# A seven-product scheme for two of the four GLU column passes in both S5 layers of a four-layer trunk

## The chip, the cores and the metric

The kernel runs on one core of a Trainium2 chip. The time is the device time of one execution in microseconds; the figure to compare is the median of several runs. The profile is one execution of its own, whose time is given beside its span below.

## What is computed

The reference is a trunk of four layers over 512 tokens of width 1024. Layers 0 and 3 use the S5 mixer, layer 1 gated linear attention, layer 2 differential attention, and every layer is followed by a SwiGLU feed-forward block (FFN). What matters here is the end of the S5 mixer, a gated linear unit (GLU):

```python
    z = jax.nn.gelu(y).astype(h.dtype)      # 512 tokens x 1024
    a, b = jnp.split(z @ w_glu, 2, axis=-1) # w_glu is 1024 x 2048
    return a * jax.nn.sigmoid(b)
...
        x = x + mix.astype(x.dtype)
        h = rmsnorm(x, norm_ffn[layer])
        x = x + swiglu_ffn(h, ffn_w_gate_up[layer], ffn_w_down[layer]).astype(x.dtype)
```

The sigmoid is computed as half of one plus a tanh of half the argument.

## The kernel before

**Numbers in two parts.** Each fp32 operand is held as a high part (a cast to fp32r, by ScalarE) and a low part (what the cast left over, by VectorE). One product of two operands is three matmuls (`mm3`): high by high, high by low, low by high. The mixer's output `zT` lies transposed in SBUF, 8 blocks of 128 rows, 512 tokens wide, both parts.

**Passes.** `w_glu` has four column groups of 512: the left ones (`a`) at 0 and 512, the gate ones (`b`) at 1024 and 1536. A pass is one `gemm_b`: four accumulators (one bank of PSUM for each 128 tokens), the inner dimension taken in four blocks of 256 rows. For every block `wb` loads 128x1024 numbers (512 KB) into a staging tile `wst` (three buffers), `high` (L368, ScalarE) and `low` (L376, VectorE) make a `whl` tile (five buffers), and 24 matmuls of 128x512 follow (L396 to L398). Pass b0 (columns 1024 to 1535) is done inside the S5 pipeline, a step behind it. `s5_glu` (L1866) then does a0, b1 and a1. `evac_b` is the tanh of the gate pass on ScalarE (L1878); `evac_a` multiplies and adds into the residual `x`, two VectorE operations for each 128 tokens (L1881, L1883).

**What follows.** `nxt` is a `Sides`, the left operand of the next FFN. `take(t, d)` takes 128 tokens and one half of the width once `x` is complete there: it lets earlier tiles go through `put` (four PE transposes, L123, then `keep`, four ScalarE scalings, L211, and after the second tile `parts`, L206 and L207) and squares the rows (L114). `flush` issues all puts that are pending. In the last pass `gemm_b` runs with `tail=4`: the last four blocks of 128 rows are done token tile by token tile, so that the tiles finish one behind another. `ahead(2)` loads and splits the first two weight blocks of the FFN ("heads"), and `total("3")` makes one of the FFN's own left sums (L225).

**The FFN's own scheme.** The FFN multiplies gate and up halves by a seven-product scheme: both operands are cut in quarters, and seven products of quarters with sums and differences of quarters take the place of eight. `seven_block` makes its sums of weights by an accumulating DMA from the POOL queue (L601) or by a VectorE addition (L658). Its first weights go to `slots`, to a `lent` tile, to `wst` and to the spare gain tile `left.g`.

**Order.** Outside `hand_all()` a planner orders each engine's instructions from the program's order and its own estimate of when they are ready. From `hand_all()` to `hand()` each engine (PE, ScalarE, VectorE, POOL and SP, which issues the DMAs) keeps the order as it is written. Each engine takes its instructions strictly in order, so a waiting one holds up those behind it. Tiles of a new pool share memory with tiles of a pool that has ended and wait until those were last used.

## Time and profile before

| what | value |
|---|---|
| runs | 2285.26, 2279.61, 2278.34 us, median 2279.61 us |
| the profiled execution | 2281.29 us, its span 2279.4 us |
| granted TensorE clock | 0.991 of full speed |
| GLU of layer 0, three passes in `s5_glu` | about 163 to 232 us of the span |
| GLU of layer 3, the same three passes | about 1861 to 1931 us of the span |
| median weight load of `w_glu` in layer 0, from issue to landing | 4.4 us |

The profile lists instructions by source line and engine, and a line may belong to a helper: L368 and L376 serve every weight split of the kernel, so one stage is read by asking for a window of time. The start times of matmuls tell their rate; their durations overlap, because the next one starts before the last has drained. What an engine waited for stands in square brackets behind its idle time.

### The profile page before, as it was taken

Reading aid. Unit: us, or ns where it says so; the run is one execution under the profiler, and the core shown is the slowest. Engines: PE = TensorE matmul, PEld = TensorE weight load, DVE = VectorE, ACT = ScalarE, POOL = GpSimd, SP = SyncE. Lnnn points to the kernel's source line nnn. Section 1 sums busy time; section 2 is a strip of 40 time slices with the busy share of each in tenths; the row PEclk is TensorE's granted clock in tenths of the full one; section 3 lists DMA queues with packets and bytes.
Section 4 is the critical chain, followed back from the end, with each engine's and each line's share of the span. In section 5 each row is a group of like instructions: output and inputs, shape, how many; then the busy total and the mean of one; then the engine's idle time right before and its main releaser. Section 6 shows DMA issues by size and latency. Waiting matters only on the chain.

```text
span 2279.4 us, 37223 instructions
## 1 busy us (share of the span) xinstructions
PE 2204.5 (97%) x14847; PEld 1956.4 (86%) x14847; DVE 1560.5 (68%) x2420; ACT 1120.6 (49%) x1870; POOL 281.6 (12%) x392
## 2 busy tenths in 40 slices
PE   5899999999999999999999999999999899999997
PEld 3778979899877799998988887999998788989896
DVE  8873887776624469777754675977766964957574
ACT  6533645454453456555535676744444234635342
POOL 1000140522000010101002231101000000101000
PEclk9999999999999999999999999999999999999999
DMA  4247475663422457765336365885631646767521
GB/s 88 46 134 194 113 188 159 181 185 99 123 65 74 131 133 202 184 166 172 96 129 145 89 150 154 238 216 135 179 94 38 159 137 157 191 161 177 154 77 65
DMA packets 295463, 317.83 MB, mean 139 GB/s; under 512 B 72221, under 2 KB 235353, under 8 KB 294906
## 3 DMA queue, kind: packets, MB, share of 16 engines
q1 hardware_dynamic: 233050, 234.23, 34.1%
q0 software_dynamic: 62240, 81.22, 19.1%
q8 instruction: 117, 1.92, 0.3%
q14 instruction: 56, 0.46, 0.1%
HBM read 283.54 MB, written 16.65 MB: 132 GB/s over the span
## 4 chain that ended last, share of the span: by engine, by line
PE 81%; DVE 9%; ACT 4%; issue 2%; DMA 2%; SPq 1%; POOL 0%; ACTq 0%; DVEq 0%; POOLq 0%
PE a L565 17%; PE acc L396 14%; PE acc L398 13%; PE acc L397 13%; PE c L565 8%; PE d L565 4%; PE y L1481 2%; DVE whl L376 2%; ACT whl L368 1%; PE V L1445 1%; PE s L2306 1%; PE op L2340 1%; PE tp L123 1%; DMA wst<-in_ffn_w_gate_up_dram 1%; DVE halves L229 1%
## 5 line engine op out<-in xcount | busy, mean ns | idle before, releaser
L376 DVE TENSOR_TENSOR whl<-wst,whl 128x1024 fp32r<-128x1024 f32 x272 | 331.6, 1224 | 260.2 <-ACT whl L368 259.4
L368 ACT CAST whl<-wst 128x1024 fp32r<-128x1024 f32 x272 | 283.9, 1050 | 310.0 <-PE acc L398 221.8
L565 PE MATMUL a<-side,whl 128*128 128x256 f32 x3168 | 382.5, 277 | 4.2 <-DVE whl L376 3.6
L565 PEld LDWEIGHTS a<-side,whl 128*128 128x128 f32 x3168 | 369.4, 188 | 6.9 <-DVE whl L376 5.3
L396 PE MATMUL acc<-whl,act 128*128 128x512 f32 x704 | 278.3, 396 | 1.3 <-DVE x L548 1.3
L397 PE MATMUL acc<-whl,act 128*128 128x512 f32 x704 | 274.7, 390 | 0.0
L398 PE MATMUL acc<-whl,act 128*128 128x512 f32 x704 | 274.6, 390 | 0.0
L565 PE MATMUL c<-side,whl 128*128 128x256 f32 x2112 | 254.3, 277 | 1.2 <-DVE whl L376 1.2
L565 PEld LDWEIGHTS c<-side,whl 128*128 128x128 f32 x2112 | 246.7, 188 | 2.0 <-DVE whl L376 2.0
L376 DVE TENSOR_TENSOR whl<-slot,whl 128x1024 fp32r<-128x1024 f32 x107 | 130.5, 1223 | 70.2 <-ACT whl L368 70.2
L396 PEld LDWEIGHTS acc<-whl,act 128*128 128x128 f32 x704 | 132.1, 188 | 31.7 <-issue 2.2
L398 PEld LDWEIGHTS acc<-whl,act 128*128 128x128 f32 x704 | 132.1, 188 | 28.1
L397 PEld LDWEIGHTS acc<-whl,act 128*128 128x128 f32 x704 | 132.2, 188 | 25.5
L368 ACT CAST whl<-slot 128x1024 fp32r<-128x1024 f32 x107 | 112.2, 1053 | 83.9 <-PE acc L398 35.1
L396 PE MATMUL acc<-whl,hT 128*128 128x512 f32 x352 | 142.8, 406 | 0.0
L398 PE MATMUL acc<-whl,hT 128*128 128x512 f32 x352 | 138.3, 393 | 0.0
L397 PE MATMUL acc<-whl,hT 128*128 128x512 f32 x352 | 138.2, 393 | 0.0
L565 PE MATMUL a<-sides,whl 128*128 128x256 f32 x1056 | 134.3, 283 | 0.0
L565 PEld LDWEIGHTS a<-sides,whl 128*128 128x128 f32 x1056 | 129.7, 191 | 1.0
L565 PE MATMUL d<-sides,whl 128*128 128x256 f32 x1056 | 126.6, 276 | 1.0 <-ACT whl L368 1.0
L565 PEld LDWEIGHTS d<-sides,whl 128*128 128x128 f32 x1056 | 122.9, 188 | 1.2 <-ACT whl L368 1.2
L704 ACT CAST act<-r 128x512 fp32r<-128x512 f32 (+1 forms) x110 | 66.3, 646 | 115.2 <-DVE r L683 107.9
(458 smaller groups left out, 3877.3 us busy)
## 6 DMA issues: line engine op xcount, KB each, us to landing
wst<-in_ffn_w_gate_up_dram SPq DMA_DIRECT2D x88, 512.0 KB, 4.8
wst<-in_ffn_w_down_dram SPq DMA_DIRECT2D x88, 512.0 KB, 4.2
slot<-in_ffn_w_gate_up_dram SPq DMA_DIRECT2D x71, 512.0 KB, 5.6
wst<-in_ffn_w_gate_up_dram POOLq DMA_DIRECT2D x44, 512.0 KB, 6.3
halves<-in_ffn_w_gate_up_dram SPq DMA_DIRECT2D x43, 512.0 KB, 5.3
wst<-in_s_w_glu_dram SPq DMA_DIRECT2D x32, 512.0 KB, 4.5
wst<-in_gla_w_in_dram SPq DMA_DIRECT2D x24, 512.0 KB, 3.6
wst<-in_diff_w_qkv_dram SPq DMA_DIRECT2D x24, 512.0 KB, 4.2
```

What stands on the lines that cost most here:

```text
L123: tr.nc.tensor.transpose(p[:, j], h[:, j * P : (j + 1) * P], tr.ident[:])
L229: v.tensor_tensor(s, s, y, op=op)
L368: self.last["high"] = self.nc.scalar.copy(hl[:, 0], w[:])
L376: self.last["low"] = self.nc.vector.tensor_tensor(hl[:, 1], w[:], hl[:, 0].bitcast(F32), op=ALU.subtract)
L396: mm(out, lh, rh, start=first, stop=False)
L397: mm(out, lh, rl, start=False, stop=False)
L398: self.last["mm"] = mm(out, ll, rh, start=False, stop=last)
L565: mm(o, hl[:, x, k, c], side[y][:, k], start=first and not (j or k or n), stop=k == 3 and n == 2, skip_group_check=True,)
L704: self.last["act high"] = nc.scalar.copy(dst[:, 0, j], src[:, j])
L1445: mm(V[kk][z][:, bs(b)], inm[:, z, bs(b)], U[:, bs(b)], start=True, stop=True)
L1481: mm(yb[:, b], q[:, j, b], om[:, j // 2, bs(b)], start=False, stop=j == 3)
L2306: nc.tensor.matmul(ss[m][:], qs[:, m, ts], ks[:, m, z], start=z == 0, stop=z == 1)
```

## The change

Pass a0 stays a pass of eight blocks of rows, now with four callbacks between its blocks. The work of b1 and a1 becomes seven products. The left operand is cut in quarters of 256 tokens by 512 inner rows (names "11", "12" for the first 256 tokens, "21", "22" for the others), the weights in quarters of 512 inner rows by 512 columns (a group, then b group).

`WideSides` makes the left sums. `whole` joins high and low parts of "21", "22" and "11" on POOL, each 128x1024 numbers ("11" in two tiles of 512). `first` to `third`, beside pass a0, make sides "1", "2" and "3", and `fourth`, behind product five, side "4". `second` also joins "12". The tile `s` of these sums is the spare gain tile, which the FFN later uses for a weight.

`seven_wide` makes the weight sums. T (`wsum`, 128x2048) is loaded, has a second quarter added by a POOL DMA, and is later changed twice by VectorE additions (`total`). Weights "3" are a staged load with an accumulating POOL DMA on top. Each product is 24 matmuls of 128x512: two token tiles, four inner blocks, three matmuls. The products run in the order one, five, six, two, seven, three, four. Results move between PSUM banks and SBUF rows r1, r5 and r2 as in the FFN's scheme. Token tiles 0 and 1 are complete before product four, tiles 2 and 3 by it. `hand_all()` now stands behind the split of weights "4".

```diff
--- before.py
+++ after.py
@@ -241,6 +241,64 @@
         for ks, y in self.of(name):
             hi, lo = (z[:, ks] for z in self.place[name])
             self.tr.nc.vector.tensor_tensor(lo, y, hi.bitcast(F32), op=ALU.subtract)
+class WideSides:
+    def __init__(self, tr, pool, hT, spare):
+        self.tr, self.hT = tr, hT
+        self.m = pool.tile([P, 4, 256], F32, name="summand")
+        self.y = {n: pool.tile([P, 2, 4, 256], F32R, name="wide" + n) for n in ("1", "4", "3", "2")}
+        self.s = spare[:].rearrange("p (k n) -> p k n", n=256)
+    def quarter(self, name, z):
+        th, kh = int(name[0]) - 1, int(name[1]) - 1
+        return self.hT[:, z, 4 * kh : 4 * kh + 4, th * 256 : (th + 1) * 256]
+    def stat(self, name):
+        y = (lambda z: self.quarter(name, z)) if len(name) == 2 else (lambda z: self.y[name][:, z])
+        return lambda k, z, t: y(z)[:, k, t * P : (t + 1) * P]
+    def joined(self, out, name, ks=slice(0, 4)):
+        hi, lo = (self.quarter(name, z)[:, ks].bitcast(F32) for z in range(2))
+        self.tr.nc.gpsimd.tensor_tensor(out, hi, lo, op=ALU.add)
+    def parts(self, name, src, ks=slice(0, 4)):
+        hi, lo = (self.y[name][:, z, ks] for z in range(2))
+        self.tr.nc.scalar.copy(hi, src)
+        self.tr.nc.vector.tensor_tensor(lo, src, hi.bitcast(F32), op=ALU.subtract)
+    def whole(self):
+        self.u = [(slice(k, k + 2), self.tr.np_.tile([P, 2, 256], F32, tag="hh", name="wideu")) for k in (0, 2)]
+        self.joined(self.s, "21")
+        self.joined(self.m[:], "22")
+        for ks, u in self.u:
+            self.joined(u[:], "11", ks)
+    def first(self):
+        v = self.tr.nc.vector
+        for ks, u in self.u:
+            v.tensor_tensor(u[:], u[:], self.s[:, ks], op=ALU.subtract)
+        v.tensor_tensor(self.s, self.s, self.m[:], op=ALU.subtract)
+        self.parts("1", self.s)
+    def second(self):
+        for ks, u in self.u:
+            self.tr.nc.vector.scalar_tensor_tensor(
+                self.s[:, ks], u[:], -1.0, self.m[:, ks], op0=ALU.mult, op1=ALU.subtract
+            )
+        self.joined(self.m[:], "12")
+        self.parts("2", self.s)
+    def third(self):
+        for ks, u in self.u:
+            self.parts("3", u[:], ks)
+    def fourth(self):
+        self.tr.nc.vector.tensor_tensor(self.s, self.s, self.m[:], op=ALU.add)
+        self.parts("4", self.s)
 
 
 class Chunks:
@@ -551,6 +609,103 @@
 
         return evac
 
+    def seven_wide(self, w, cols, sums, T, four, r2):
+        nc = self.nc
+        v = nc.vector
+        mm = nc.tensor.matmul
+        piece = lambda q, half, b: self.wb_src(w, 4 * q + 2 * b, cols[half])
+        r1, r5 = four[:2], four[2:]
+        a, c = ([self.acc() for z in range(2)] for y in range(2))
+        f = {"r1": r1, "r5": r5, "a": a}
+        H = {}
+        def load(q, half, plus=None):
+            out = []
+            for b in range(2):
+                y = self.staged(piece(q, half, b), 2, 512)
+                if plus:
+                    nc.gpsimd.dma_start(y[:], piece(*plus, b), accum_op=ALU.add)
+                out.append(y)
+            return out
+        def split(name, ys):
+            H[name] = [self.halves(y, 2, 512) for y in ys]
+        cut = lambda b: T[:, 2 * b : 2 * b + 2]
+        def total(q, half):
+            for b, y in enumerate(load(q, half)):
+                v.tensor_tensor(cut(b), cut(b), y[:], op=ALU.add)
+        def product(side, name, bank, first, tiles=(0, 1), ks=slice(0, 4)):
+            st = sums.stat(side)
+            for t in tiles:
+                for k in range(4)[ks]:
+                    hl = H[name][k // 2]
+                    for n, (x, y) in enumerate(((0, 0), (0, 1), (1, 0))):
+                        mm(
+                            bank[t][:], st(k, x, t), hl[:, y, k % 2], start=first and not (k or n),
+                            stop=k == 3 and n == 2, skip_group_check=True,
+                        )
+        for b in range(2):
+            nc.sync.dma_start(cut(b), piece(0, 1, b))
+            nc.gpsimd.dma_start(cut(b), piece(0, 0, b), accum_op=ALU.add)
+        split("11", load(0, 0))
+        def one():
+            split("1", [cut(0), cut(1)])
+            product("11", "11", a, True)
+            for z in range(2):
+                nc.scalar.copy(r1[z][:], a[z][:])
+        def five():
+            total(1, 1)
+            split("2", [cut(0), cut(1)])
+            product("1", "1", c, True)
+            for z in range(2):
+                nc.scalar.copy(r5[z][:], c[z][:])
+        def six():
+            split("21", load(1, 0))
+            product("2", "2", a, False)
+            for z in range(2):
+                nc.scalar.copy(r2[z][:], a[z][:])
+        def two():
+            d = [self.sbank("d") for z in range(2)]
+            split("3", load(0, 1, (1, 1)))
+            product("12", "21", d, True)
+            for z in range(2):
+                v.tensor_tensor(r1[z][:], r1[z][:], d[z][:], op=ALU.add)
+        def seven():
+            split("22", load(1, 1))
+            product("3", "3", a, False)
+        def seven_out(z):
+            v.tensor_tensor(r5[z][:], r5[z][:], a[z][:], op=ALU.subtract)
+        def three():
+            total(1, 0)
+            product("4", "22", c, False)
+        def three_out(z):
+            v.tensor_tensor(r2[z][:], c[z][:], r2[z][:], op=ALU.subtract)
+        def four_weights():
+            split("4", [cut(0), cut(1)])
+        def four(z, ks=slice(0, 4)):
+            product("22", "4", a, False, (z,), ks)
+        return dict(
+            f, one=one, five=five, six=six, two=two, seven=seven, seven_out=seven_out, three=three, three_out=three_out,
+            four=four, **{"four weights": four_weights},
+        )
 
     def seven_product(self, side, w, bank, first, hl=None):
 
@@ -1870,28 +2025,58 @@
         wg = self.i["s5_w_glu"][L]
         nxt = Sides(self, 3 * L, self.i["ffn_w_gate_up"][3 * L])
         with self.tc.tile_pool(name=f"s5g_{L}", bufs=1) as p:
-            for d in range(2):
-                gate = [None] * NT
-
-                def evac_b(t, ps):
-                    gate[t] = p.tile([P, 512], F32, tag="gate", name="gate", bufs=6)
-                    nc.scalar.activation(gate[t][:], ps[:], AF.Tanh, scale=0.5)
-
-                def evac_a(t, ps):
-                    v.scalar_tensor_tensor(gate[t][:], gate[t][:], 1.0, ps[:], op0=ALU.add, op1=ALU.mult)
-                    xs = self.x[:, t, d * 512 : (d + 1) * 512]
-                    v.scalar_tensor_tensor(xs, gate[t][:], 0.5, xs, op0=ALU.mult, op1=ALU.add)
-                    nxt.take(t, d)
-
-                stat = lambda k, part, t: zT[:, part, k, t * P : (t + 1) * P]
-                if d == 0:
-                    for t in range(NT):
-                        evac_b(t, accs[t])
-                else:
-                    self.gemm_b(stat, wg, KT, D + d * 512, evac_b)
-                ahead = (lambda: (nxt.ahead(2), nxt.total("3"))) if d else None
-                with nullcontext() if d else self.tc.issue_after(self.last_turned.ins):
-                    self.gemm_b(stat, wg, KT, d * 512, evac_a, tail=4 if d else 0, ahead=ahead)
+            self.edge(p, 64)
+            row = lambda tag, bufs: p.tile([P, 512], F32, tag=tag, name=tag, bufs=bufs)
+            gate = [row("gate", 4) for t in range(NT)]
+            low2 = [row("r2", 2) for z in range(2)]
+            sums = WideSides(self, p, zT, nxt.g)
+            T = p.tile([P, 4, 512], F32, name="wsum")
+            for t in range(NT):
+                nc.scalar.activation(gate[t][:], accs[t][:], AF.Tanh, scale=0.5)
+            def gated(t, d, th, value):
+                v.scalar_tensor_tensor(th, th, 1.0, value, op0=ALU.add, op1=ALU.mult)
+                xs = self.x[:, t, d * 512 : (d + 1) * 512]
+                v.scalar_tensor_tensor(xs, th, 0.5, xs, op0=ALU.mult, op1=ALU.add)
+            def evac_a(t, ps):
+                gated(t, 0, gate[t][:], ps[:])
+                nxt.take(t, 0)
+            stat = lambda k, part, t: zT[:, part, k, t * P : (t + 1) * P]
+            with self.tc.issue_after(self.last_turned.ins):
+                self.gemm_b(stat, wg, KT, 0, evac_a, between=(sums.whole, sums.first, sums.second, sums.third))
+            f = self.seven_wide(wg, (512, D + 512), sums, T, [row("gate", 4) for z in range(4)], low2)
+            tanh = lambda y: nc.scalar.activation(y, y, AF.Tanh, scale=0.5)
+            f["one"]()
+            self.flush()
+            f["five"]()
+            sums.fourth()
+            f["six"]()
+            f["two"]()
+            f["seven"]()
+            for z in range(2):
+                f["seven_out"](z)
+                tanh(f["r5"][z][:])
+            f["three"]()
+            for z in range(2):
+                f["three_out"](z)
+                tanh(low2[z][:])
+                gated(z, 1, low2[z][:], f["r1"][z][:])
+            nxt.take(0, 1)
+            f["four weights"]()
+            self.hand_all()
+            nxt.ahead(2)
+            nxt.total("3")
+            f["four"](0)
+            nxt.take(1, 1)
+            gated(2, 1, f["r5"][0][:], f["a"][0][:])
+            f["four"](1, slice(0, 2))
+            nxt.take(2, 1)
+            f["four"](1, slice(2, 4))
+            gated(3, 1, f["r5"][1][:], f["a"][1][:])
+            nxt.take(3, 1)
         return nxt
 
 
```

## Prediction

> **What bounds the kernel now.** I read the page first, its busy line and its chain, and then went to the two GLU stages by windows.
>
> ```profile
> span 2279.4 us, 37223 instructions
> PE 2204.5 (97%) x14847; PEld 1956.4 (86%) x14847; DVE 1560.5 (68%) x2420; ACT 1120.6 (49%) x1870; POOL 281.6 (12%) x392
> PE 81%; DVE 9%; ACT 4%; issue 2%; DMA 2%; SPq 1%; POOL 0%; ACTq 0%; DVEq 0%; POOLq 0%
> 163.00:185.00 22.00, 22.00 (x99) 18.21 (x98) 9.59 (x9) 7.80 (x10) 0.00 (x0) 1.00 0.58 179
> 185.00:209.00 24.00, 23.98 (x115) 19.69 (x114) 9.66 (x12) 13.06 (x32) 0.15 (x1) 1.00 0.46 146
> 209.00:232.00 23.00, 23.00 (x107) 19.03 (x106) 7.95 (x11) 8.03 (x18) 4.95 (x4) 1.00 1.15 269
> 1907.00:1931.00 24.00, 24.00 (x114) 19.86 (x113) 8.57 (x11) 8.76 (x20) 5.18 (x4) 1.00 0.98 220
> PE acc L396 <- ACT zT L1494: 0.7, 1, 0.7
> ```
> PE is busy for 97% of the span and holds 81% of the chain. In the three passes of layer 0 (163 to 232 us) and the last one of layer 3 it is busy throughout at full clock. The last line is all that PE waited for in layer 0 between 160.8 and 232.2 us: 0.7 us, at the very start. VectorE (third pair of columns) is busy for 8 to 10 us of each 22 to 24, ScalarE for 8 to 13, POOL for hardly anything. So these stages are bound by the number of matmuls. What one costs is its distance to the next, not its duration:
>
> ```profile
> 217.82 0.39 PE L397 MATMUL acc<-whl,zT 128*128 128x512 f32 x1
> ...
> 225.53 0.40 PE L398 MATMUL acc<-whl,zT 128*128 128x512 f32 x1
> 225.76 0.60 PE L123 MATMUL tp<-ident,x 128*128 128x128 f32 x4
> 226.12 0.48 PE L396 MATMUL acc<-whl,zT 128*128 128x512 f32 x1
> ...
> 232.17 0.60 PE L123 MATMUL tp<-ident,x 128*128 128x128 f32 x4
> 232.52 3.11 PE L565 MATMUL a<-sides,whl 128*128 128x256 f32 x24
> ...
> 250.26 2.78 PE L565 MATMUL a<-side,whl 128*128 128x256 f32 x22 [0.19 <-DVE whl L376]
> ```
> From 217.82 to 225.53 us start 35 matmuls, 34 steps: 7.71 / 34 = 0.2268 us each. Four transposes of a token tile (L123) take 0.36 us of PE. The last of them before the FFN start at 232.17, the FFN's first product at 232.52. The bracket shows that PE first waits, for 0.19 us, at 250.26: the FFN's start has little room on VectorE.
>
> **What the change removes.** b1 and a1 are 192 matmuls, seven products are 7 x 24 = 168, of the same 128x512 form. 24 x 0.2268 = 5.44 us a layer, **10.9 us** for both. That is the most it can bring. The transposes stay.
>
> **What it adds on ScalarE and VectorE.** The durations:
>
> ```profile
> L376 DVE TENSOR_TENSOR whl<-wst,whl 128x1024 fp32r<-128x1024 f32 x14 | 17.1, 1224 | 29.2 <-ACT whl L368 29.2
> L368 ACT CAST whl<-wst 128x1024 fp32r<-128x1024 f32 x14 | 14.6, 1051 | 26.5 <-PE acc L398 22.8 <-DMA wst<-in_s_w_glu_dram 3.7
> L1881 DVE SCALAR_TENSOR_TENSOR gate<-gate,acc 128x512 f32<-128x512 f32 x7 | 4.7, 686 | 8.8 <-PE acc L398 8.8
> L1883 DVE SCALAR_TENSOR_TENSOR x<-gate,x 128x512 f32<-128x512 f32 x7 | 4.7, 690 | 0.1
> L1878 ACT ACTIVATE gate<-acc 128x512 f32<-128x512 f32 x8 | 4.6, 601 | 2.6 <-PE acc L398 2.3
> L114 ACT ACTIVATE sq<-x 128x512 f32<-128x512 f32 x7 | 4.4, 630 | 8.6 <-DVE x L1883 8.6
> L211 ACT ACTIVATE halves<-tp,gffn 128x128 f32<-128x128 f32 x24 | 6.8, 373 | 2.4 <-PE tp L123 2.4
> L225 DVE TENSOR_TENSOR s<-halves 128x512 f32<-128x512 f32 x2 | 1.3, 686 | 0.0
> 160.67 0.69 DVE L1497 TENSOR_TENSOR zT<-zp,zT 128x512 fp32r<-128x512 f32 x1 [8.28 <-ACT zT L1494]
> 161.62 2.36 DVE L376 TENSOR_TENSOR whl<-wst,whl 128x1024 fp32r<-128x1024 f32 x2 [0.26 <-ACT whl L368]
> 246.04 0.68 DVE L644 TENSOR_TENSOR r<-r,d 128x512 f32<-128x512 f32 x1
> 246.64 1.22 DVE L658 TENSOR_TENSOR lent<-lent,slot 128x1024 f32<-128x1024 f32 x1
> 180.34 1.05 ACT L368 CAST whl<-wst 128x1024 fp32r<-128x1024 f32 x1 [4.38 <-PE acc L398]
> ```
> Weight splits: 14 in place of 8, each 1.05 us of ScalarE and 1.22 of VectorE. VectorE from the first split of a0 (161.6) to the start of product four: the last GLU matmuls end at 232.17 - 5.44 = 226.7, product four and two puts take 5.44 + 0.72, so it starts at 220.6, and each earlier product 5.44 us before the next. 18 splits (4 for a0) x 1.22 = 22.0; left sums 2 x 0.69 + 1.22, + 2 x 0.69, + 1.22, and their low parts 4 x 1.22 or a little more, 10.2; four additions to T x 1.22 (as L658 on `lent`) 4.9; six evacuations x 0.68 (as L644, which also reads PSUM) 4.1; the gating of a0 4 x 1.38 = 5.5; one tile behind it 1.4; one `parts` 1.2. Sum 49.3 us in 59.0, or 84%. ScalarE has less: 18 x 1.05, four sides x 1.05, six copies and four tanhs x 0.6, four tanhs more of pass b0, 11 of squares and puts (L114, L211): 43. Both fit, and the L368 row of 180.34 us shows how far ahead splits run now: it had waited 4.38 us for PE to free a `whl`, not the reverse. A product holds two of the five `whl`, so the next two can be made while it runs for 5.44 us, against some 3.5 for two splits. The copies of r1, r5 and r2 and the subtraction of seven each lie beside a product on other banks. I cost all this at **nothing**. If the cover went, each VectorE instruction of 1.22 us that is late costs PE 1.22.
>
> **POOL.** The joins are four additions of 128x1024, which no row shows. The nearest:
>
> ```profile
> L1193 POOL MEMSET in<- 64x512 f32 x2 | 1.0, 519 | 0.1
> L1037 POOL TENSOR_SCALAR nident<-ident 128x128 fp32r<-128x128 f32 x1 | 0.6, 551 | 0.1
> L1093 POOL MEMSET r<- 128x4 f32 x8 | 0.8, 105 | 111.6 <-ACT r L1092 111.6
> L601 POOL DMA_DIRECT2D wst<-in_ffn_w_gate_up_dram x44 | 57.6, 1308 | 418.3 <-DMA wst<-in_ffn_w_gate_up_dram 127.0 <-DVE slot L658 70.2 <-DVE x L548 61.2
> DMA to landing us min/median/max: 5.7/6.9/11.7
> ```
> A memset of 512 columns takes 0.52 us (two of them), so 1.04 for 1024; a one-input operation on 128 columns takes 0.55, so at that rate 4.4. I take 3.6, near the latter, which is the one that reads SBUF (0.55 less the 0.1 that a memset of four columns takes, times eight): 10.8 us for three joins from 161.4 us, where the last low part of `zT` ends (L1497), done by about 172 (bounds 165 and 175). Side "1" is used by product five from 220.6 - 5 x 5.44 = 193.4 us on, and what lies between (three VectorE operations or splits and a cast, 5 us) fits. In POOL's queue the two accumulating DMAs of T stand behind these joins at worst; each is issued in 1.3 us and landing takes 6.9 us in the median, so T is whole at about 182 and split by 186, seven us before product five. Cost **nothing**; with joins at the upper bound it is still 4 us early.
>
> The Trainium skill ("GPSIMD Engine Reference", section 3.1) has 4497 ns for such an addition of 2048 columns, so about 2.25 us for 1024, an estimate from that page; the sum would be the same.
>
> **DMAs.** 14 loads in place of 8 and 4 accumulating ones, so 10 x 0.5 MB more a layer.
>
> ```profile
> wst<-in_s_w_glu_dram SPq DMA_DIRECT2D x9, 512.0 KB, 4.4
> wst<-in_ffn_w_gate_up_dram POOLq DMA_DIRECT2D x2, 512.0 KB, 10.7
> wst<-in_ffn_w_gate_up_dram SPq DMA_DIRECT2D x5, 512.0 KB, 5.8
> slot<-in_ffn_w_gate_up_dram SPq DMA_DIRECT2D x5, 512.0 KB, 14.3
> 194.85 6.61 SPq L357 DMA_DIRECT2D wst<-in_ffn_w_gate_up_dram  x2
> 201.51 0.50 SPq L598 DMA_DIRECT2D slot<-in_ffn_w_gate_up_dram  x1
> ```
> The tight place is weights "3". They keep two of three `wst` buffers from the load until the accumulation has landed. The second of them waits for the buffer of weights "21a", which is split only when product one frees a `whl`: 192 (193.4 less four puts of 0.36), plus 1.05 and 1.22, some 195 us with a busy VectorE. From there load L, accumulation A and a split (2.27) must be done when product seven, which starts at 209.7, reaches its second half of inner rows, 5.44 / 4 later: 211.0. L + A may be 13.7 us. With 4.4 and 6.9 they are 11.3: 2.4 us of room. With the 5.8 and 10.7 that the FFN's loads and accumulations had in this stage they are 16.5, and PE waits 2.8. I take **0**, since fewer transfers are in flight here than there, and keep 2.8 for the range.
>
> **The handover to the FFN** is where I see a loss. Now the heads are loaded from 194.85 us on, the first slot at 201.51, 31 us before use. Afterwards the second head waits for the `wst` of the last `total`, about 216 us, and the slots stand behind it on SP: with 5.8 us to landing the first is there at 222, with the 14.3 of a slot at 231, and it is used at about 229. The room goes from 30 us to a few, but suffices. Worse is VectorE's written order: gating of tiles 0 and 1, both heads' low parts, `total("3")` (L225), and then gating of tile 2, behind which PE's transposes and the FFN's first product stand. From the end of product three: subtraction 0.68, tanh 0.60, gating 1.38, two splits 2.44, two subtractions of 0.69 each, gating 1.38, together 7.9 us. PE has product four, 5.44, and eight transposes, 0.72: 6.2. It waits **1.7 us a layer**. Bounds: 0, if a head's split comes earlier, and 3.5, if the second head or the first slot is two us late as well. What follows in the FFN is then shifted as a whole.
>
> **The sum.** Against the profiled execution's own 2281.29 us (span 2279.4, 1.9 us around it): 2 x (5.44 - 1.7) = 7.5 us, so 2273.8. The median of the runs shown is 2279.61, 1.7 less; carried to it, the prediction is **2272.1 us**, a gain of 0.33%, the size that a measurement of this kernel can just tell from no change (0.3%, 6.8 us).
>
> **Rivals.**
> *Part of the gain is lost to late operands.* The handover at its bound of 3.5 us, or weights "3" late by 2.8, leaves 2 x (5.44 - 3.5) = 3.9 or 2 x (5.44 - 1.7 - 2.8) = 1.9 us: 2276 to 2278. For: 2.4 us of room only, in a stage that moves more bytes. Against: splits run 4.4 us ahead today.
> *Slower: weights "3" starve product seven.* The same chain with the slowest values: a slot's 14.3 us for L, 11.7 (the slowest accumulation) for A, 26.0 in place of 13.7. PE would wait 12.3 us a layer: 2 x (12.3 + 1.7 - 5.44) = 17.1, so 2297. It ends slower by over 0.3% from L + A = 13.7 + 3.74 + 3.4 = 20.8 us. Those values come from the FFN's bursts of many loads at once; here `wst` lets three be in flight beside T.
> *VectorE and POOL exclude each other.* If VectorE stood still during joins, it would have 49.3 + 4 x 3.6 = 63.7 us of work in 59.0: 4.7 late, 2 x (4.7 + 1.7 - 5.44) = +1.9, so 2282; with joins of 4.4, 7.9 late, +8.3, so 2288; with joins of 1.04 nothing is lost. No row of this trace has a POOL operation of that size beside VectorE.
> The Trainium skill ("SBUF — State Buffer", section "Who interferes with whom") states this rule: a VectorE instruction with two SBUF inputs and a GpSimd one that reads SBUF lock each other out. No run here shows it yet.
> *The change doesn't do what it says*, if matmuls come out no fewer, or the planner sets the products behind waits of its own: no gain, 2280.
>
> **How the numbers follow.** Forecast (gain of 6.9 to 10.9) 0.46; part lost 0.28; starved 0.13; exclusion 0.10, of which 0.06 within 0.3% and 0.04 slower; not as said 0.03. So faster 0.46, same 0.28 + 0.06 + 0.03 = 0.37, slower 0.13 + 0.04 = 0.17. The range goes from no wait at all, 2279.6 - 10.9 = 2268.7, less some scatter, 2268, to 2284, past the partial cases and the middle of exclusion; only starved and worst excluded runs, some 0.17, lie above.
>
> **What would show it.** 48 fewer matmuls of 128x512 on PE; at their step of 0.2268 the FFN's first product of layer 0 at about 232.5 - 5.4 + 1.7 = 228.8 us. A PE wait on x or VectorE's L1883 ahead of the last transposes shows the handover; a wait on a `whl` split in product seven, with ScalarE waiting on a POOL DMA of `wst`, shows "3"; L376 well over 1.22 us during the joins shows exclusion. The prediction is wrong if PE waits in the middle products, or if the FFN's first blocks lose more than the handover does.

## The result: 0.6% slower

The changed kernel takes 2295.82 us in the median (2293.41 to 2299.95), the kernel before 2281.62 in the same comparison; the ratio is 1.0062, 95% interval [1.0047, 1.0077], so about 14 us slower where 7.5 us faster was predicted. Its profiled execution took 2299.95 us with a span of 2297.9, that is 18.5 us more than the span before.

Its page, first line, busy line and shares of the chain:

```profile
span 2297.9 us, 37310 instructions
PE 2206.2 (96%) x14799; PEld 1953.1 (85%) x14799; DVE 1616.0 (70%) x2474; ACT 1145.8 (50%) x1904; POOL 313.6 (14%) x410
PE 75%; DVE 13%; ACT 4%; DMA 4%; issue 3%; POOL 0%; SPq 0%; ACTq 0%; DVEq 0%; POOLq 0%
```
14847 - 14799 = 48 matmuls are gone, as the change says. PE's share of the chain fell from 81 to 75%, VectorE's rose from 9 to 13 and that of the DMAs from 2 to 4: PE waits where it did not.

Where it waits is in the timeline of PE in layer 0 (start, duration, instruction, and in brackets the idle time before it and who ended that; only rows with a wait, and the starts of stages):

```profile
185.20 0.39 PE L456 MATMUL acc<-whl,zT 128*128 128x512 f32 x1
189.85 0.76 PE L649 MATMUL acc<-whl,zT 128*128 128x512 f32 x1 [4.27 <-DVE gate L2038]
191.01 1.09 PE L123 MATMUL tp<-ident,x 128*128 128x128 f32 x4 [0.39 <-DVE x L2040]
...
200.50 11.14 PE L649 MATMUL acc<-whl,wide 128*128 128x512 f32 x48
...
220.18 0.50 PE L649 MATMUL acc<-whl,wide 128*128 128x512 f32 x1 [1.74 <-ACT whl L426]
221.44 9.57 PE L649 MATMUL acc<-whl,wide 128*128 128x512 f32 x41 [0.76 <-DVE whl L434]
...
236.57 0.66 PE L123 MATMUL tp<-ident,x 128*128 128x128 f32 x4 [2.64 <-DVE x L2040]
...
240.17 1.11 PE L123 MATMUL tp<-ident,x 128*128 128x128 f32 x4 [0.61 <-DVE x L2040]
...
244.27 3.11 PE L720 MATMUL a<-sides,whl 128*128 128x256 f32 x24
```
The first pass ends at 185.4 us, within 0.2 us of where it ended before. Then there are three places of waiting: ahead of product one (4.27 + 0.39), inside product seven (1.74 + 0.76), at the handover (2.64 + 0.61): 10.4 us in all, in a stretch in which PE of the kernel before waited for nothing. The FFN's first product starts at 244.27 us, before it was 232.52.

The same stretch by windows (stretch, its sum, then busy time of PE, PEld, DVE, ACT and POOL, the granted clock, the DMA share and GB/s):

```profile
186.00:189.80 3.80, 0.00 (x0) 0.00 (x0) 3.77 (x5) 1.04 (x1) 0.00 (x0) 0.97 0.44 130
189.80:193.00 3.20, 2.75 (x10) 2.13 (x11) 3.20 (x6) 1.84 (x6) 0.00 (x0) 0.50 0.59 175
193.00:196.00 3.00, 3.00 (x9) 2.42 (x8) 2.04 (x3) 2.60 (x10) 1.19 (x1) 0.50 0.09 12
196.00:199.70 3.70, 3.70 (x16) 2.96 (x16) 0.96 (x1) 1.81 (x4) 0.00 (x0) 0.94 0.89 136
236.60:240.20 3.60, 2.99 (x11) 1.93 (x11) 3.60 (x7) 2.21 (x7) 1.93 (x2) 0.61 1.09 348
240.20:244.20 4.00, 4.00 (x13) 3.31 (x14) 1.15 (x2) 3.53 (x9) 1.27 (x1) 0.50 1.16 263
```
After the first and the last of the three waits the granted clock is 0.50 for 6.8 us each. At 0.50 matmuls of this form start 0.43 us apart in place of 0.227 (read in the run with nine additions below), so in a window with clock c I count PE's busy time b as work of b x c, and b x (1 - c) as lost: 1.38, 1.50 and 0.22 us behind product one's wait, 1.17 and 2.00 behind the handover's, 6.3 us together. Waits and clock are 16.7 us; less the 5.44 of the missing matmuls that is 11.2, and measured were 244.27 - 232.52 = 11.75. In layer 3 the same waits appear (2.30 + 0.69, 1.40 + 0.76, 2.31 + 1.57), 9.0 us, with half clock behind the first only. By the table below the stage lost 11.9 us in layer 0 and 6.4 in layer 3: 18.3 of the 18.5 us by which the two profiled spans differ.

### The profile page after: what moved, and what is told of

It is laid out like the page before. It is cut to its first block, busy times and chain, and to the rows that moved or that the text cites. A ratio compares the mean times of both kernels' runs of the same rounds, so it can differ in the third digit from the quotient of the medians.

```text
span 2297.9 us, 37310 instructions
## 1 busy us (share of the span) xinstructions
PE 2206.2 (96%) x14799; PEld 1953.1 (85%) x14799; DVE 1616.0 (70%) x2474; ACT 1145.8 (50%) x1904; POOL 313.6 (14%) x410
## 4 chain that ended last, share of the span: by engine, by line
PE 75%; DVE 13%; ACT 4%; DMA 4%; issue 3%; POOL 0%; SPq 0%; ACTq 0%; DVEq 0%; POOLq 0%
PE a L720 17%; PE acc L454 11%; PE acc L456 11%; PE acc L455 11%; PE c L720 8%; PE d L720 4%; DVE whl L434 3%; DMA wst<-in_s_w_glu_dram 2%; PE y L1636 2%; ACT whl L426 2%; PE V L1600 1%; PE s L2491 1%; PE acc L649 1%; PE op L2525 1%; PE tp L123 1%
## 5 line engine op out<-in xcount | busy, mean ns | idle before, releaser
L434 DVE TENSOR_TENSOR whl<-wst,whl 128x1024 fp32r<-128x1024 f32 x272 | 332.9, 1230 | 210.7 <-ACT whl L426 210.1
L434 DVE TENSOR_TENSOR whl<-slot,whl 128x1024 fp32r<-128x1024 f32 x107 | 130.5, 1222 | 69.6 <-ACT whl L426 69.6
```

Source lines behind the costliest of these rows:

```text
L434: self.last["low"] = self.nc.vector.tensor_tensor(hl[:, 1], w[:], hl[:, 0].bitcast(F32), op=ALU.subtract)
```

## Who is late: three queues

**Product one.** The rows of VectorE ahead of it:

```profile
184.35 1.23 DVE L271 TENSOR_TENSOR wide<-spare,wide 128x1024 fp32r<-128x1024 f32 x1
185.49 1.22 DVE L641 TENSOR_TENSOR wsum<-wsum,wst 128x1024 f32<-128x1024 f32 x1
186.63 1.22 DVE L434 TENSOR_TENSOR whl<-wsum,whl 128x1024 fp32r<-128x1024 f32 x1
187.88 1.22 DVE L641 TENSOR_TENSOR wsum<-wsum,wst 128x1024 f32<-128x1024 f32 x1
189.03 1.28 DVE L2038 SCALAR_TENSOR_TENSOR gate<-gate,acc 128x512 f32<-128x512 f32 x2
```
The gating of a0 (L2038) frees the accumulators that product one needs. It begins at 189.03, 3.6 us after the pass is done, and VectorE did not rest before it. It made the low part of left side "4" (L271, for product three), a low part of T (L434, for product five) and the two additions to T (L641). These are written down in `five`, but their result is the weights "2", which product *six* uses. The planner had put all of them ahead of the gating. This is a matter of order, not of load: after it, VectorE has time (before 198.74 and before 203.53 us it waits 3.7 and 3.6 us for ScalarE).

**Product seven.** Rows of ScalarE, GpSimd and SP around the weights "3" (timelines of the three, in the order named):

```profile
200.39 2.18 ACT L211 ACTIVATE halves<-tp,gffn 128x128 f32<-128x128 f32 x8
202.39 1.11 ACT L426 CAST whl<-wsum 128x1024 fp32r<-128x1024 f32 x1
...
204.00 2.00 ACT L426 CAST whl<-wst 128x1024 fp32r<-128x1024 f32 x2
...
219.08 2.94 ACT L426 CAST whl<-wst 128x1024 fp32r<-128x1024 f32 x3 [6.82 <-DMA wst<-in_s_w_glu_dram]
...
210.84 1.18 POOL L630 DMA_DIRECT2D wst<-in_s_w_glu_dram  x1 [15.68 <-DMA wst<-in_s_w_glu_dram]
...
206.34 16.58 SPq L415 DMA_DIRECT2D wst<-in_s_w_glu_dram  x5
```
Read them by time. Product five starts at 200.5, behind product one; ScalarE does eight put operations and a split of T, and only then the split of weights 21, whose buffer the second load of "3" waits for. SP gives that load out at 206.34, it has landed when GpSimd issues the accumulation at 210.84 (4.5 us), and that has landed when ScalarE's split begins at 219.08 (8.2 us). Load and accumulation are 12.7 us. The last row shows a second effect: SP needed 16.6 us to give out five loads, because they stood waiting for `wst` buffers. The last two of them are for T's last additions, and the FFN's weights stand behind them.

**The handover.** VectorE again:

```profile
232.35 0.68 DVE L697 TENSOR_TENSOR r<-acc,r 128x512 f32<-128x512 f32 x1
232.96 1.22 DVE L434 TENSOR_TENSOR whl<-wst,whl 128x1024 fp32r<-128x1024 f32 x1
234.09 0.69 DVE L2038 SCALAR_TENSOR_TENSOR r<-r,gate 128x512 f32<-128x512 f32 x1
234.69 1.22 DVE L434 TENSOR_TENSOR whl<-wst,whl 128x1024 fp32r<-128x1024 f32 x1
235.82 0.69 DVE L2040 SCALAR_TENSOR_TENSOR x<-r,x 128x512 f32<-128x512 f32 x1
```
The heads' two low parts (L434) stand between the two gating steps of token tile 0 (L2038, L2040), at whose end (236.5) PE's transposes start. VectorE was late here already. The subtraction at 232.35 (L697) reads a bank that product three had filled by about 228.1 us (product four starts at 230.85, 12 matmuls earlier is 228.1). Ahead of it VectorE waited for loads of `w_glu`:

```profile
225.75 1.23 DVE L641 TENSOR_TENSOR wsum<-wsum,wst 128x1024 f32<-128x1024 f32 x1 [1.50 <-DMA wst<-in_s_w_glu_dram]
...
228.34 1.23 DVE L641 TENSOR_TENSOR wsum<-wsum,wst 128x1024 f32<-128x1024 f32 x1 [0.77 <-DMA wst<-in_s_w_glu_dram]
```
These are T's last additions, and their loads are the two that SP gave out last, after 221.4 us.

## The experiments

For each run the median and its ratio to the kernel before with the interval; the two last columns are read from each profile, layer 0 / layer 3: us from the end of the first GLU pass (start of its last matmul plus 0.23) to the first product of the FFN. With 5.44 us less than before, they would be 41.5. A profiled execution is not always near its kernel's median: the changed kernel's took 2299.95 us and that of "gating first" 2288.08, 11.9 us apart where the medians are 3.3 apart.

| kernel | median us | ratio to before | layer 0 | layer 3 |
|---|---|---|---|---|
| before | 2280.95 to 2282.15 (medians) | 1 | 46.9 | 46.9 |
| changed | 2295.82 | 1.0062 [1.0047, 1.0077] | 58.8 | 53.3 |
| gating first | 2292.57 | 1.0044 [1.0026, 1.0061] | 49.3 | 50.7 |
| no joins | 2291.69 | 1.0052 [1.0031, 1.0072] | 50.2 | 55.2 |
| handover reordered | 2293.59 | 1.0056 [1.0037, 1.0075] | 51.5 | 48.4 |
| own tile only | 2285.60 | 1.0021 [1.0012, 1.0031] | 50.8 | 49.1 |
| gating first + own tile | 2275.64 | 0.9974 [0.9964, 0.9984] | 43.5 | 43.4 |
| the same + handover | 2274.35 | 0.9970 [0.9960, 0.9979] | 43.0 | 41.6 |
| gating first + own tile, no joins | 2277.19 | 0.9973 [0.9961, 0.9985] | 43.1 | 44.6 |

### One cause at a time

**Gating first.** The first pass's last gating is put ahead of the T additions written in `five` and of the fourth left sum:

```diff
-                v.tensor_tensor(cut(b), cut(b), y[:], op=ALU.add)
+                with self.tc.issue_after(self.gate_last.ins):
+                    v.tensor_tensor(cut(b), cut(b), y[:], op=ALU.add)
...
-            sums.fourth()
+            with self.tc.issue_after(self.gate_last.ins):
+                sums.fourth()
```
`gate_last` is the last VectorE operation of that gating.

> The changed kernel with one edit: the two VectorE additions to T behind the first split of T (`total` of five) and the making of side 4 (`fourth`) may only follow the gating of pass a0 on VectorE. Theory Q (order): the gating of a0 stands behind VectorE work that nobody needs yet (side 4 and T's first total, 4.9 us), so PE idles 4.3 us (layer 0) and 2.3 us (layer 3) ahead of product one and then runs at half clock for some microseconds. By Q both gaps fall under 1 us and the half-clock stretch behind them goes: about -7.5 us in layer 0 and -4 in layer 3, so some 2285 where the changed kernel had 2296. Rival P (VectorE has too much to do, POOL's joins holding it up): the moved operations are late further on, products five or six wait instead, and under 3 us are gained. Rival D (weights 3 set the pace): the wait ahead of the second half of product seven (2.5 us a layer now) grows by what is gained before it.

2292.57 us. In both layers the wait ahead of product one is gone, and with it the half clock behind it. But the wait in product seven grew, and brought a half clock of its own. PE of this kernel, and a window behind the second row:

```profile
210.31 0.50 PE L650 MATMUL acc<-whl,wide 128*128 128x512 f32 x1 [2.61 <-ACT whl L426]
...
1915.08 0.80 PE L650 MATMUL acc<-whl,wide 128*128 128x512 f32 x1 [4.19 <-ACT whl L426]
```
```profile
1916.00:1918.00 2.00, 1.66 (x4) 1.39 (x5) 2.00 (x4) 0.92 (x1) 0.00 (x0) 0.50 0.32 49
```
So the weights "3" were the next bound, hidden behind the first wait: with PE earlier at product seven, a chain that ends at its own time is waited for longer. In layer 3 the waits ahead of product one and in product seven were 5.2 us together and are 4.7 now; in layer 0 they fell from 7.2 to 3.4. The handover's waits fell too, to 0.87 + 0.89 and 0.87 us. In time, the interval of this run overlaps with the changed kernel's, and so do those of the next two: what each of these three is worth alone, the medians do not tell.

**No joins.** The left side's sums are taken from the high part alone, copied by ScalarE, and GpSimd adds nothing.

```diff
-        self.tr.nc.gpsimd.tensor_tensor(out, hi, lo, op=ALU.add)
+        self.tr.nc.scalar.copy(out, hi)
```

> The changed kernel with the left sums made from the high parts alone: ScalarE copies take the place of POOL's joins, the low parts are left out of the sums. Rival P (POOL's joins and VectorE exclude each other): the stretched VectorE rows (3.5 us for two of 0.64 in layer 0, 4.5 for two of 1.2 and 2.9 for one of 0.68 in layer 3) go back to their plain length, VectorE reaches the gating of a0 earlier, and the gap ahead of product one closes nearly whole: -6 to -10 us in all. Theory Q (order): the gating stays behind the same operations, so the gap falls by no more than the stretch, 2.2 us, in each layer, and the total by some 3 to 5 us.

2291.69 us. In layer 0 the wait ahead of product one shrank from 4.27 to 0.62 us, so the joins had their part in pushing VectorE's work to that moment there. In layer 3 it was 2.93 us, so they are not its cause. The other two waits stayed (1.73 + 0.77 and 1.27 + 0.75 us in product seven, 3.4 us each at the handover).

**Handover reordered.** The FFN's first weights are asked for ahead of the output of product three, the gating of tiles 0 to 2 comes ahead of the heads' low parts, and T's last total goes to the end:

```diff
             f["three"]()
+            f["four weights"]()
+            self.hand_all()
+            heads = [self.staged(nxt.quarter(0, 0, b), 4, 256) for b in range(2)]
...
-            nxt.ahead(2)
-            nxt.total("3")
             f["four"](0)
...
+            for z in range(2):
+                self.low(nxt.heads[z], heads[z])
...
+            nxt.total("3")
             nxt.take(3, 1)
```

> The changed kernel with the written order of the handover changed alone: hand_all() stands ahead of product three's outputs, VectorE gates tiles 0, 1 and 2 first and then splits the heads, total 3 comes last. Theory H (order at the handover): PE's waits for x ahead of the transposes (2.6 + 0.6 us in layer 0, 2.3 + 1.6 + 0.3 in layer 3) fall under 1 us a layer, and in layer 0 the half clock behind them (some 7 us long, 3.4 us lost) goes: about -6 us in layer 0, -3.5 in layer 3. Rival (the FFN's first weights come too late, because their loads start 30 us later than before): the waits turn into waits of the FFN's first products for splits of heads or slots, and under 3 us are gained in all.

2293.59 us. The handover's wait fell to 1.30 and 1.28 us and no half clock followed; but waits of 0.76 to 0.83 us for FFN weights appear behind it. This is what its rival expected.

**Own tile only.** The second half of the weights "3" gets a tile of its own, so that its load and accumulation go early and take no `wst` buffer:

```diff
+        nc.sync.dma_start(own[:], piece(0, 1, 1))
+        nc.gpsimd.dma_start(own[:], piece(1, 1, 1), accum_op=ALU.add)
...
-            split("3", load(0, 1, (1, 1)))
+            y = self.staged(piece(0, 1, 0), 2, 512)
+            nc.gpsimd.dma_start(y[:], piece(1, 1, 0), accum_op=ALU.add)
+            split("3", [y, own])
```

> The changed kernel with the tile of its own for the second half of product three's weights alone; the gating stays behind the T additions and the handover is as changed. Theory (both stalls are real and add): product one's wait of 2.3 to 4.3 us and the half clock behind it, about 3.2 us, stay in both layers, so 6 us a layer more than with the gating first as well (2275.6): about 2288 us, product seven without a wait or with one under 0.8 us. Rival 1 (the chain of product three's weights was the whole loss): 2276 to 2279 us. Rival 2 (late gating delays the chain too, so the wait in product seven comes back): 2291 to 2296 us.

2285.60 us, between the theory and its first rival, and clear of the changed kernel. Product seven has no wait any more; product one waited even longer (layer 0; 4.03 us in layer 3):

```profile
188.10 0.76 PE L649 MATMUL acc<-whl,zT 128*128 128x512 f32 x1 [5.44 <-DVE gate L2043]
```
So late gating does not make the weights late by itself once half of them have their own place (the second rival falls).

### Causes together

**Gating first + own tile.**

> The changed kernel with (1) the first pass's gating put ahead of the T additions of product five and of the fourth sum, as in the run before, and (2) the second half of the weights of product three in a tile of its own (4 KB of a partition), loaded and accumulated by the DMA early, so that of the late chain only one 2-tile load and accumulation is left. Theory (the wait of 3.4 to 4.7 us in product seven is this chain of load, accumulation and split): the wait in product seven goes to under 1 us in both layers, 3 us less in layer 0 and 5 less in layer 3 than with the gating alone (2292.6): about 2285 us. Rival (the chain is held by its start, behind product one's copies and the low halves of sums 2 and 1, not by its length): the wait stays over 2 us and the time within 2290 to 2293. Either way the handover wait remains (0.9 to 2.6 us and what may follow it in the clock).

2275.64 us, 9 us better than expected and faster than the kernel before. PE of layer 0:

```profile
205.27 5.60 PE L650 MATMUL d<-whl,zT 128*128 128x512 f32 x24
210.71 11.04 PE L650 MATMUL acc<-whl,wide 128*128 128x512 f32 x48
...
227.26 0.66 PE L123 MATMUL tp<-ident,x 128*128 128x128 f32 x4 [0.94 <-DVE x L2046]
```
Products two, seven and three (24 + 48 matmuls) run without a gap. The handover's wait is smaller too, 0.94 us in place of 2.64 + 0.61 in layer 0 and 1.16 in place of 2.31 + 1.57 in layer 3, though nothing there was touched. Either mend alone had done much of this (gating first: above; own tile only: 0.47 and 1.15 us). SP shows what changed:

```profile
201.37 7.81 SPq L415 DMA_DIRECT2D wst<-in_s_w_glu_dram  x4
211.71 2.10 SPq L415 DMA_DIRECT2D wst<-in_ffn_w_gate_up_dram  x2
```
In the changed kernel SP stood with GLU loads until 222.9 us (206.34 + 16.58); here the last is out at 209.2. So T's last additions come earlier (the second at 213.93 us, without a wait), and VectorE's first subtraction behind product three starts 0.8 us after its bank is full, at 219.67, in place of 4.2. The FFN's own weights are not the reason: their first loads go out 17.8 us ahead of the FFN's first product here (211.71 to 229.50) and 20.0 in the changed kernel (224.28 to 244.27). That the shorter queue on VectorE shortens the wait is read from these rows; no run changes it alone.

**The same + handover.**

> As the run with its own tile, and the handover in another order as well: the feed-forward stage's first weights asked for and split ahead of product three's output, first gating by tiles, T total last. Theory (three waits, each with its own cause, add up to the loss): product one's, seven's and the handover's waits all under 1 us, 2 x 2 us less than the kernel with the own tile alone: about 2281 us, the kernel before's time or a little under. Rival (taking one wait away only feeds the next, VectorE and ScalarE setting the end): 2285 to 2292 us, with the waits moved into the feed-forward's first products.

2274.35 us, 7.8 less than the kernel before in the same comparison (2282.15). Whether it beats the run above is open: 1.3 us, and the intervals overlap. In layer 3 the whole saving arrives at the FFN:

```profile
1880.32 0.39 PE L456 MATMUL acc<-whl,zT 128*128 128x512 f32 x1
...
1922.14 3.11 PE L725 MATMUL a<-sides,whl 128*128 128x256 f32 x24
```
From 1880.55 to 1922.14 are 41.6 us, 5.3 less than the 46.9 before. In the FFN some of it goes again, to a wait of 0.76 us for weights that VectorE has not split.

**Gating first + own tile, no joins.**

> The kernel with the gating first and the own tile, with GpSimd's joins of the left side's sums left out (ScalarE copies the high part alone, so the second of the two left parts is missing from the rounded sums). Theory (with the queue mended the joins lie beside the matmuls and cost nothing, as the prediction had it): 2275.6 us, within 1 us. Rival (GpSimd's additions still stretch VectorE's work, or their lateness moves it): 2270 to 2273 us. If ScalarE, at 9 of 10 parts busy in places, is the tight engine: 2277 to 2279 us, since the copies are ScalarE's.

2277.19 us, the same within the interval; it lies nearest to the third case, but is not told apart from the theory. That VectorE and GpSimd hinder each other is plain in the rows all the same. The pair of low parts L271, with the joins (first VectorE, then GpSimd, of the changed kernel; with both mends the pair takes 3.50 us):

```profile
173.76 3.49 DVE L271 TENSOR_TENSOR wide<-wideu,wide 128x512 fp32r<-128x512 f32 x2
...
173.99 2.72 POOL L266 TENSOR_TENSOR summand<-zT 128x1024 f32<-128x1024 f32 x1 [6.09 <-DVE spare L289]
```
and without them:

```profile
171.19 1.28 DVE L271 TENSOR_TENSOR wide<-wideu,wide 128x512 fp32r<-128x512 f32 x2
```
2.2 us more for the pair, but it lies beside the first pass's matmuls and costs no time. The Trainium skill ("SBUF — State Buffer", "Who interferes with whom") has VectorE instructions with two SBUF inputs and GpSimd's reads shut each other out; these rows agree, and the time shows no cost of it in the mended kernel.

### The half clock by itself

Is the slow clock a result of the wait, or of something else in the changed kernel? In the kernel *before*, n more additions on VectorE (gate = 0 x accumulator + gate) are put ahead of the gating of a0's first tile, and the other tiles' gating behind it:

```diff
                 def evac_a(t, ps):
+                    if d == 0 and t == 0:
+                        for _ in range(9):
+                            v.scalar_tensor_tensor(gate[t][:], ps[:], 0.0, gate[t][:], op0=ALU.mult, op1=ALU.add)
```

A first form, which added into a tile of its own and left the additions to the planner's order, told nothing:

> The kernel before with nine extra VectorE additions of 128x512 (a row of SBUF and the first accumulator of pass a0, 0.68 us each, result unused) ahead of the first gating of pass a0 in both S5 layers: 6.1 us later, so PE idles about 4.7 us ahead of pass b1 where it had no gap. Theory C (an idle PE of that length is followed by a stretch at half clock): each layer loses the 4.7 us and some 3 more at a granted clock of 0.5, 15 us in all. Rival (the half clock in the changed kernel has another cause, such as its instruction mix): the clock stays at 1.0 and 9.5 us are lost.

2279.75 us, ratio 0.9994 [0.9984, 1.0004]: the planner put the gating of the other tiles between the additions, PE never stood, and there was no clock to look at. With the order forced:

> The kernel before, with nine extra additions (gate = 0 x accumulator + gate, VectorE, about 0.60 us each) ahead of the gating of the first row tile of the first column pass in each S5 layer, and the other three tiles' gating put behind it: the product after it cannot begin before the first tile's accumulator is free, so TensorE should stand still for about 9 x 0.60 + 0.7 + 0.3 - 9 x 0.227 = 4.4 us in each of the two layers. Clock theory (a wait of more than about 2.3 us is followed by some 6.5 us of half clock, about 3.2 us lost): 2 x (4.4 + 3.2) = 15 us more than before, 2296 us; granted clock 0.5 in the two windows of 3 us behind the wait, matmuls 0.45 us apart. Rival (the half clock behind product one's wait came from something else, POOL or the transfers of the changed kernel): 2 x 4.4 = 9 us more, 2290 us, clock 1.0 behind the wait.

> The same with five additions: TensorE should stand still for about 5 x 0.60 + 0.7 + 0.3 - 2.04 = 2.0 us in each layer. Clock theory with its bound near 2.3 us: no half clock, 2 x 2.0 = 4 us more, 2285 us. If shorter waits already take the clock down: 2291 us and 0.5 in the windows behind the wait. If the wait is made up elsewhere: 2281 us.

> The kernel before with three extra additions ahead of the first gating: with five TensorE stood still 3.47 us, with nine 6.37 us, so 0.725 us for each, and with three about 2.0 us in each layer. Clock theory with a bound between 2.3 and 2.6 us: clock 1.0 behind the wait, 2 x 2.0 = 4 us more than before, 2286 us. If a wait of 2.0 us also takes the clock down, 2290 us and windows at 0.5. (Five additions cost 9.2 us, nine 17.0.)

PE's row behind the wait with nine, five and three additions, and a window behind each:

```profile
192.34 0.77 PE L396 MATMUL acc<-whl,zT 128*128 128x512 f32 x1 [6.37 <-DVE gate L1886]
...
194.00:196.00 2.00, 2.00 (x10) 1.90 (x9) 2.00 (x4) 1.92 (x9) 0.00 (x0) 0.50 0.04 8
```
```profile
187.54 0.77 PE L396 MATMUL acc<-whl,zT 128*128 128x512 f32 x1 [3.47 <-DVE gate L1886]
...
188.00:190.00 2.00, 2.00 (x8) 1.56 (x8) 2.00 (x4) 1.34 (x4) 0.00 (x0) 0.50 0.71 240
```
```profile
186.69 0.47 PE L396 MATMUL acc<-whl,zT 128*128 128x512 f32 x1 [1.01 <-DVE gate L1886]
...
188.00:190.00 2.00, 2.00 (x15) 1.70 (x14) 2.00 (x4) 2.00 (x8) 0.00 (x0) 1.00 0.03 8
```
Nine cost 2299.16 - 2282.15 = 17.0 us, where the two waits are 12.7; five cost 9.2 us (ratio 1.0040 [1.0027, 1.0054]), where the waits are 6.9; three, with waits of 1.01 us and the clock at 1.00 in the windows behind them, cost nothing that is measured (1.0009 [0.9998, 1.0019]). So waits of 3.47 and 6.37 us are followed by half clock in a kernel that has nothing else of the change, and cost about 1 and 2 us more than themselves. The rival, another cause than the wait, falls for waits of this length. The expectation for five was wrong in its length, 3.47 us in place of 2.0, and that for three in the other direction; a wait of 2 us was not made this way.

## Why the prediction was wrong, step by step

**What the change removes** was right. 48 matmuls are gone at 0.2268 us each; with all three mends layer 3 takes 41.6 us to the FFN where the full saving would give 41.5. The gain is real, and the changed kernel spends it three times over in layer 0 (16.7 us against 5.44).

**What it adds on ScalarE and VectorE, "at nothing"**: this step failed. The count of work was no underestimate (49.3 us; VectorE was busy for 43.1 from 161.6 us to the start of product four), but a mean load of 84% does not say that the one instruction PE needs next is served next. Work for products three, five and six stood ahead of the gating that frees product one's banks: 4.27 us in layer 0, 2.30 in layer 3. The prediction named the price (each late VectorE instruction costs PE 1.22) but assumed an order by need. The run with gating first shows that order is the cause of this wait: the same instructions, no wait. The rival "the planner sets the products behind waits of its own" was nearest to this, but at 2280 us and a chance of 0.03 for all of its kind it had neither the size nor the weight.

**Weights "3"**: the sizes were right, the start was not. Load and accumulation took 12.7 us where up to 13.7 was allowed. The chain was to start at 195 us and started at 206.3. Product five started at 200.5 instead of 193.4; and between that and the split of weights 21 ScalarE had puts, copies and a split of T, which the prediction had not counted in this chain. With gating first the second part remains: the wait is then 2.61 and 4.19 us. The rival "weights 3 starve product seven" (2297 us) had one of the three places right. That its time is close to the measured one is luck: it has a wait of 12.3 us from transfers of 26 us, where 2.5 us of wait and 12.7 of transfers were measured.

**The handover** had the kind of wait right, the heads' low parts ahead of the gating, and the waits lay within its bounds in layer 0 (2.64 + 0.61 against 0 to 3.5) but not in layer 3 (2.31 + 1.57). It had the wrong place: PE waited for tiles 0 and 1, not for tile 2. The value taken, 1.7, lets VectorE begin when product three ends; in fact it was behind by then, with T's last additions that had waited for the stalled GLU loads and a low part of T (1.22 us at 231.22) that the sum does not have there.

**No step had the clock.** The sum counted waits at their length. Half clock behind them cost 6.3 us more in layer 0, more than the whole saving of that layer. The granted clock was 1.00 in all the windows that the prediction shows, and PE had no wait of this length in them. The Trainium skill ("TensorE: Matmul & The Clock Gate", section "Why this matters for your kernels") warns of gaps over about 3 us; the runs with 3.47 and 6.37 us agree, and gaps of 2.30 to 2.64 us did it here too.

**GpSimd's joins**: cost nothing that could be measured, as the prediction said, once the rest is mended; they took 2.4 to 3.4 us in place of 3.6. The rival that they and VectorE exclude each other was right as to the rows. In the changed kernel as it was, the joins had a share in layer 0's first wait; whether by the exclusion or by being late, no run separates.

With gating, own tile and handover mended, the kernel takes 7.8 us less than before, where 7.5 was forecast for the kernel as written; with the first two alone 6.5. That the figures meet is in part luck: the forecast has a wait of 1.7 us a layer at the handover, and the mended kernel has 0.29 there and other short waits elsewhere.

## What to carry to other kernels

Before costing added work at nothing by an engine's mean load, list what stands in its queue at the moments when PE needs something of it, above all where the planner may pull later work forward because its operands are there. Expect several waits in series to hide each other, and mend them together before judging a change: by the medians each mend alone gave under 11 us here, none enough to pass the kernel before, and two together 20. Here a load that waited for a staging buffer held up every load behind it on SP, so 4 KB of a partition for the slowest one paid twice: in product seven and at the handover.

## Not expected of the hardware

The length of a wait did not decide whether the clock fell. A wait of 2.30 us (and one of 0.69 behind it) in layer 3 of the changed kernel brought 0.50, while 2.31 us at that layer's handover and 2.24 us with the handover reordered left it at 1.00; 1.73 us followed by 0.77 brought 0.50 in the run with no joins, while 1.74 followed by 0.76 in the changed kernel did not.

Read in windows of 0.5 us, the half clock has a length and a place of its own. Seven traces have it in these two stages, 15 times in all, and each time it lasted 3.41 or 6.83 us, which is twice that: after the same wait of 3.47 us with five additions, 3.41 in layer 0 and 6.83 in layer 3. Within one trace all its starts and ends lie on one grid: those of the changed kernel, at 189.58, 196.41, 237.37, 244.19, 1899.66 and 1903.07 us, are whole multiples of 3.413 us apart, to 0.02 us.

What decided in these stages was how long PE stood still between two steps of that grid. Four such steps of layer 3 of the changed kernel, two and two (PE's busy time is behind the comma, the clock third from the end):

```profile
1896.24:1899.65 3.41, 1.50 (x10) 1.19 (x11) 3.41 (x7) 1.15 (x4) 0.00 (x0) 1.00 0.73 235
1899.65:1903.07 3.42, 3.42 (x11) 2.74 (x10) 3.00 (x5) 2.81 (x12) 1.12 (x1) 0.50 0.08 32
...
1940.61:1944.02 3.41, 1.58 (x9) 1.41 (x10) 3.41 (x6) 1.60 (x5) 0.00 (x0) 1.00 1.02 318
1944.02:1947.44 3.42, 1.85 (x11) 1.28 (x10) 2.57 (x5) 2.03 (x8) 1.30 (x1) 1.00 1.09 349
```
In the first PE stood still for 3.41 - 1.50 = 1.91 us, and the next step has half clock; in the third it was 1.83 us, and the clock stays. In the seven traces every step at full clock with 1.91 us of rest or more was followed by half clock, and none with 1.84 or less. So a wait of 2.3 us can go either way, by where it falls on the grid. Rest is not all that counts: elsewhere, at 674.27 us of the changed kernel, the clock fell after 3.27 us in which PE was busy throughout.
